# Two-layer encoder on one core: the cross-attention's output projection tile by tile with parity blocks, the MLP's Strassen operands from transposed tiles, and a hand-written order for the up-projection

## The chip, the cores and the metric

The kernel runs on one core of one Trainium2 chip, in one launch. The metric is the device time in microseconds. A core has TensorE (PE: matmuls and transposes, with the weight load PEld beside it), VectorE (DVE), ScalarE (ACT), GpSimd (POOL) and SyncE (SP, whose queue issues nearly all transfers here). Each engine works through its own queue in order and waits there on semaphores of the others; PSUM has eight banks of 128x512 f32 that PE writes and DVE or ACT read.

## The reference

An encoder of two layers over 1024 tokens of width 1024. Layer 0 mixes tokens by attention, layer 1 by pooling; each layer then cross-attends into 256 memory tokens and ends in a gated MLP of inner width 2816 with a convolution of width 3 along the tokens. The part that the change touches:

```python
def memory_cross_attention(h, mem_n, w_q, w_kv, w_o):
    ...
    o = jnp.einsum('bhsm,bmhd->bshd', p, v).reshape(b, s, D_MODEL)
    return o @ w_o

def conv_gated_ffn(h, w_up, conv_w, conv_b, w_down):
    u = h @ w_up
    up = jnp.pad(u, ((0, 0), (1, 1), (0, 0)))
    u = up[:, :-2] * conv_w[0] + up[:, 1:-1] * conv_w[1] + up[:, 2:] * conv_w[2] + conv_b
    gate, val = u[..., :D_FF], u[..., D_FF:]
    return (jax.nn.silu(gate) * val) @ w_down
...
        x = x + memory_cross_attention(rmsnorm(x, xattn_norm[i]), rmsnorm(mem, mem_norm[i]),
                                       xattn_w_q[i], xattn_w_kv[i], xattn_w_o[i])
        x = x + conv_gated_ffn(rmsnorm(x, ffn_norm[i]), ffn_w_up[i], ffn_conv_w[i],
                               ffn_conv_b[i], ffn_w_down[i])
```

## The kernel before

**Products.** All matrices are float32. `hi_lo` splits an operand in two reduced parts: ACT writes the high part (L153), DVE subtracts it to get the low part (L154). `mm3` multiplies two split operands with three matmuls, high by high, high by low and low by high (L233, L234, L235). The parts live in `R`, 20 tiles that are given out whole or by halves; raw data and intermediate results live in six `scr` tiles. `psB` hands out single PSUM banks in turn, `psA` pairs of banks.

**Stages of a layer.** Mixer; `cross`, which ends with the transposed attention output `O` in blocks of four token tiles; output projection; up-projection; down-projection. The residual `X` is eight tiles of 128 tokens by 1024 channels.

**Output projection (`project`, L248).** An outer loop goes over the two halves `n` of 512 output columns, an inner one over the eight token tiles `t`. A step is eight `mm3` into one bank and a DVE add into `X` (L261). The weight half is loaded and split at the start of its `n`. In the second round each finished tile gets `first(t)`: a DMA of the raw residual to DRAM (`Xd<-X`, L723) and the RMS norm in place (L219); one tile later `second(t)` prepares the operands of the MLP.

**Operands of the up-projection (`seven_into`, L706).** For each pair f of 22, the gate block f and the value block 22 + f of 128 columns each are computed together as a 2 by 2 block product in Strassen's form as modified by Winograd: seven products instead of eight. On the token side, the blocks of X are split by first and last four token tiles and by lower and upper 512 channels; on the weight side, the blocks are A11, A12, A21, A22. In the code's names, p1 = A11·B11, p2 = A12·B21, p3 = S4·B22, p4 = A22·T4, p5 = S1·T1, p6 = S2·T2, p7 = S3·T3. B and T blocks are made from X in row layout: subtractions first (L733, two on DVE and two on POOL, with a tile `extra`), then every block is transposed on PE (`turn`, L718) and split. T3 and T4 are turned after the projection (`tail`). That makes 112 transposes of 128x128 a layer. The S blocks are sums of weight blocks, made by POOL (L782 to L785).

**Up-projection (`ffn`, `ffn_main`).** `load(f)` brings the two 512 KB weight blocks of pair f (L771). A product is four `mm3`, so twelve matmuls (`product`). The bank `z` holds p1, then p6, p7 and p4 on top of it; the bank `y` holds p5, then p3. After each product its bank is read into `u`: p2 is copied by ACT (L811), p1 is added by DVE (L817), p5 and p6 are copied by ACT (p6's at L879), p3 is added (L885), p7 is added (L890), p4 is copied by ACT (L896). `z` may not be continued before it has been read. Then the width-3 convolution runs over u: centre tap on ACT (L841), left and right taps on DVE (L842, L843); SiLU on ACT (L887); the gate product on DVE (L902); the result G goes to DRAM (L903). Pair f's products are written in the order p1, p5, p6, p3, p7, p2 of pair f + 1, p4, with `ahead()` placing the splits of pair f + 1 between them. The order in which the engines get all this is set by the framework's scheduler, in the projection and in the whole up-projection.

**Down-projection (L910 to L938).** It reads G back and multiplies in rounds of four blocks. It starts once the up-projection has ended.

Of the kernel before, what the change touches and what calls it, by code (L numbers as in the profile page):

```python
# [16 lines left out]
P = 128  # L17
# [13 lines left out]
XH = 4  # L31
# [49 lines left out]
class Slots:  # L81
# [31 lines left out]
    def hv(self, h):  # L113
        return self.tiles[h[0]][:, h[1] * 1024:(h[1] + 1) * 1024]


class Kernel:
# [504 lines left out]
    def cross(self, i, hT, qT, ws):  # L622
# [19 lines left out]
        def scores(t):  # L642
# [19 lines left out]
            if t % 4 == 3:  # L662
                for h in range(XH):
                    R.put(qT[h, half])

        def turn(t):
            if t % 4 == 0:
                PT[t // 4] = [R.get() for _ in range(4)]
            self.transposed(prs.pop(t), self.put_T(PT[t // 4], t))
# [17 lines left out]
        for t in range(4):  # L687
            scores(t)
            memory_part(4 + t)
        for t in range(4):  # L690
            scores(4 + t)
            turn(t)
        values(0, (0, 1))
        turn(4)
        values(0, (2, 3))
        turn(5)
        turn(6)
# [8 lines left out]
    def seven_into(self, X, gain, Xd):  # L706

        nc, R = self.nc, self.R  # L710
        H = {}

        def turn(name, t, src):
            if name not in H:
                H[name] = [R.get(), R.get()]
            p = self.psB().rearrange("p (a b) -> p a b", a=4)
            for k in range(4):
                nc.tensor.transpose(p[:, k, :], src[:, k * P:(k + 1) * P], self.ident)  # L718
            h, l = (R.v(s, 4)[:, :, (t % 4) * P:(t % 4 + 1) * P] for s in H[name])
            self.hi_lo(h, l, p)  # L720

        def first(t):
            nc.sync.dma_start(out=Xd[t * P:(t + 1) * P, :], in_=X[t])  # L723
            self.normed(X[t], gain, X[t])

        def second(t):
            lo, hi = slice(0, 512), slice(512, 1024)
            if t < 4:
                turn("B11", t, X[t][:, lo])
                turn("B21", t, X[t][:, hi])  # L730
                return
            x, y = X[t - 4], X[t]
            sub = lambda e, out, p, q: e.tensor_tensor(out=out, in0=p, in1=q, op=OP.subtract)  # L733
            sub(nc.vector, x[:, lo], y[:, lo], x[:, lo])
            t2 = self.extra
            sub(nc.vector, t2, y[:, hi], x[:, lo])
            sub(nc.gpsimd, y[:, lo], y[:, hi], y[:, lo])
            sub(nc.gpsimd, x[:, hi], x[:, hi], t2)
            turn("B22", t, y[:, hi])
            turn("T1", t, x[:, lo])  # L740
            turn("T2", t, t2)

        def tail():
            for t in range(4, NT):
                turn("T3", t, X[t][:, :512])
            for t in range(4, NT):
                turn("T4", t, X[t - 4][:, 512:])
        return (first, second), H, tail

    def ffn(self, i, H, X, Xd):  # L750
        nc, R, a = self.nc, self.R, self.a
# [4 lines left out]
        cp = self.psB()[:, :4 * 2 * NF].rearrange("p (j f) -> p j f", j=4)  # L756
        for j in range(4):
            nc.tensor.transpose(cp[:, j, :], c3[:, j, :], self.ident[:2 * NF, :2 * NF])
        cv = self.cst.tile([P, 4, 2 * NF], F32, name="conv")
        nc.vector.tensor_copy(cv, cp)  # L760
        wu, wd = a["ffn_w_up"][i], a["ffn_w_down"][i]
        G = self.tc.dram_tile([FF, S], F32, name=f"G{i}")
        raws, ops, bank = {}, {}, {}
        spare = []

        def load(f):

            tiles = [spare.pop(0) for _ in range(4)] if spare else [self.scr() for _ in range(4)]
            for j, c in ((0, f), (1, NF + f)):
                src = wu[:, c * P:(c + 1) * P].rearrange("(k p) n -> p k n", p=P)  # L770
                nc.sync.dma_start(out=tiles[j].rearrange("p (k n) -> p k n", k=NK), in_=src)  # L771
            raws[f] = tiles

        def blocks(f):
            g, v, s, u = raws[f]
            return {"A11": g[:, :512], "A12": g[:, 512:], "A21": v[:, :512], "A22": v[:, 512:],
                    "S1": s[:, :512], "S2": s[:, 512:], "S3": u[:, :512], "S4": u[:, 512:]}

        def sums(f):
            b = blocks(f)  # L780
            tt = nc.gpsimd.tensor_tensor
            tt(out=b["S1"], in0=b["A21"], in1=b["A22"], op=OP.add)  # L782
            tt(out=b["S2"], in0=b["S1"], in1=b["A11"], op=OP.subtract)
            tt(out=b["S4"], in0=b["A12"], in1=b["S2"], op=OP.subtract)
            tt(out=b["S3"], in0=b["A11"], in1=b["A21"], op=OP.subtract)  # L785

        def halves(h):
            return R.hv(h)[:, :512], R.hv(h)[:, 512:]

        def split(f, name):  # L790
            h = ops[f, name] = R.get_half()
            self.hi_lo(*halves(h), blocks(f)[name])

        def done(f):
            if f:
                spare.extend(raws[f])
            del raws[f]

        def product(f, left, right, out, start):

            ah, al = (x.rearrange("p (k n) -> p k n", k=4) for x in halves(ops[f, left]))
            bh, bl = (R.v(s, 4) for s in H[right])
            for k in range(4):
                self.mm3(out, ah[:, k], al[:, k], bh[:, k], bl[:, k], start and k == 0, k == 3, not start)
            R.put_half(ops.pop((f, left)))

        def p2(f):
            x = self.psB()
            product(f, "A12", "B21", x, True)
            u = bank[f] = {"g": self.scr()}  # L810
            nc.scalar.copy(u["g"][:, :512], x)  # L811

        def p1(f):
            u = bank[f]
            z = u["z"] = self.psB()
            product(f, "A11", "B11", z, True)
            nc.vector.tensor_tensor(out=u["g"][:, :512], in0=z, in1=u["g"][:, :512], op=OP.add)  # L817

        load(0)
        sums(0)  # L820
        for n in ("A12", "A11", "S1", "S2"):
            split(0, n)

        def go():
            p2(0)
            p1(0)

        return go, lambda late, tail: self.ffn_main(H, X, Xd, late, tail, cv, G, wd, spare, load, sums, split, done,
                                                    product, p1, p2, bank)

    def ffn_main(self, H, X, Xd, late, tail, cv, G, wd, spare, load, sums, split, done, product, p1, p2, bank):
        nc, R = self.nc, self.R
        tail()
        for n in ("S4", "S3", "A22"):
            split(0, n)
        done(0)
        spare.extend(X[t] for t in (4, 5, 6, 7, 0, 1, 2, 3))

        def conv(u, f):
            c = self.scr()  # L840
            nc.scalar.activation(c, u, AF.Identity, scale=cv[:, 1, f:f + 1], bias=cv[:, 3, f:f + 1])  # L841
            nc.vector.scalar_tensor_tensor(c[:, 1:], u[:, :S - 1], cv[:, 0, f:f + 1], c[:, 1:], op0=OP.mult, op1=OP.add)  # L842
            nc.vector.scalar_tensor_tensor(c[:, :S - 1], u[:, 1:], cv[:, 2, f:f + 1], c[:, :S - 1], op0=OP.mult, op1=OP.add)  # L843
            return c
# [12 lines left out]
        order = ("A12", "A11", "S1", "S2", "S4", "S3", "A22")  # L857
        load(1)
        sums(1)
        for f in range(NF):  # L860
            u, left = bank[f], list(order)

            def ahead(n=1):
                for _ in range(n):
                    if f + 1 < NF:
                        if left:
                            split(f + 1, left.pop(0))
                            if not left:
                                done(f + 1)
                    elif first:  # L870
                        operand(*first.pop(0))

            if f:
                p1(f)
                ahead()
            z, y = u["z"], self.psB()
            product(f, "S1", "T1", y, True)
            u["v"] = self.scr()
            nc.scalar.copy(u["v"][:, 512:], y)  # L879
            ahead()  # L880
            product(f, "S2", "T2", z, False)
            nc.scalar.copy(u["g"][:, 512:], z)
# [22 lines left out]
        for s in H.values():  # L905
            R.put(*s)
# [239 lines left out]
```

## Time and profile before

| | |
|---|---|
| time, median of 3 runs | 2661.28 us (2661.01 to 2662.27) |
| time of the profiled execution | 2661.13 us |
| span of the profile | 2659.4 us |
| PE busy | 2595.0 us, 98% |
| DVE, ACT, POOL busy | 1720.5, 1207.8, 695.0 us |
| mean granted clock of TensorE | 0.992 |

In layer 0, the output projection and the first pairs of the up-projection run from 846 us to 1055 us of the span and the rest of the up-projection up to 1389 us; in layer 1 the same stages begin at about 1925 us. A row of the timeline gives the start, the duration, the engine, the line, the operation, output and input with their shapes, and in brackets how long the engine was idle before it and what ended that. Busy time is no start-to-start time: DVE and ACT begin an instruction before the one ahead has fully ended, and PE's matmuls overlap. So what an instruction takes of its queue is read as the distance of two starts. The granted clock is the share of TensorE's full clock in a stretch.

### The profile page before, as it was taken

How to read it: one execution, taken by the hardware profiler on the slowest of the kernel's cores; microseconds unless marked ns; L12 is line 12 of the kernel's file. 1: busy time of each engine (PE TensorE's matmuls, PEld its weight loads, DVE VectorE, ACT ScalarE, POOL GpSimd, SP SyncE). 2: the span in 40 equal slices, each digit the busy share in tenths (PEclk: the TensorE clock that was granted, in tenths of full speed). 3: DMA queues.
4: the chain of work that ended last, by engine and by line, in shares of the span. 5: the costliest groups of instructions: out<-in, count | busy, mean ns of one | idle time of the engine just before them, and what ended most of it. 6: DMA issues, size and time to landing. Idle time of an engine off the chain costs nothing.

```text
span 2659.4 us, 36296 instructions
## 1 busy us (share of the span) xinstructions
PE 2595.0 (98%) x13913; PEld 2216.8 (83%) x13913; DVE 1720.5 (65%) x2291; ACT 1207.8 (45%) x2024; POOL 695.0 (26%) x709
## 2 busy tenths in 40 slices
PE   8989999999999999999999998999999999999998
PEld 7988888888898878888878888889878888887886
DVE  6779999955246387777765435425378777767434
ACT  4448888843135255454542205425245555444111
POOL 3664445521012153433300001102034333310001
PEclk9999999999999999999999999999999999999999
DMA  4200000032222132223254203322122232326201
GB/s 157 83 1 1 1 1 1 2 135 65 70 80 89 48 95 73 94 72 95 87 187 154 100 19 89 103 64 72 58 92 91 72 95 72 95 104 241 99 24 63
DMA packets 167554, 209.22 MB, mean 79 GB/s; under 512 B 6741, under 2 KB 134077, under 8 KB 167381
## 3 DMA queue, kind: packets, MB, share of 16 engines
q1 hardware_dynamic: 167381, 206.91, 23.4%
q8 instruction: 109, 1.79, 0.3%
q14 instruction: 64, 0.52, 0.1%
HBM read 166.42 MB, written 35.65 MB: 76 GB/s over the span
## 4 chain that ended last, share of the span: by engine, by line
PE 57%; DVE 2%; ACT 2%; DMA 1%; issue 1%; POOL 1%; SPq 0%; POOLq 0%; DVEq 0%; ACTq 0%
PE pB L234 18%; PE pB L233 18%; PE pB L235 18%; DVE R L154 1%; ACT R L153 1%; DMA scr<-X 0%; DMA scr<-G 0%; PE pA L998 0%; PE pA L233 0%; PE pA L234 0%; PE pA L235 0%; DVE scr L842 0%; PE pB L718 0%; POOL ms L206 0%; DVE scr L843 0%
## 5 line engine op out<-in xcount | busy, mean ns | idle before, releaser
L233 PE MATMUL pB<-R,R 128*128 128x512 f32 (+1 forms) x3088 | 1160.9, 377 | 16.5 <-ACT scr L879 9.6
L234 PE MATMUL pB<-R,R 128*128 128x512 f32 (+1 forms) x3088 | 1157.6, 375 | 4.3 <-DVE R L154 4.0
L235 PE MATMUL pB<-R,R 128*128 128x512 f32 (+1 forms) x3008 | 1125.6, 374 | 0.0
L233 PEld LDWEIGHTS pB<-R,R 128*128 128x128 f32 x3088 | 582.1, 189 | 127.6 <-ACT scr L879 10.4
L234 PEld LDWEIGHTS pB<-R,R 128*128 128x128 f32 x3088 | 582.7, 189 | 109.0 <-DVE R L154 7.5
L235 PEld LDWEIGHTS pB<-R,R 128*128 128x128 f32 x3008 | 567.5, 189 | 101.0 <-DVE R L154 0.4
L153 ACT ACTIVATE R<-scr 128x1024 fp32r<-128x1024 f32 (+1 forms) x186 | 185.7, 1024 | 353.0 <-PE pB L234 283.5
L154 DVE TENSOR_TENSOR R<-X,R 128x512 fp32r<-128x512 f32 x294 | 256.3, 885 | 63.6 <-ACT R L153 63.0
L153 ACT ACTIVATE R<-X 128x512 fp32r<-128x512 f32 x294 | 181.3, 630 | 245.4 <-PE pB L234 225.6
L922 DVE TENSOR_TENSOR X<-pB,X 128x512 f32<-128x512 f32 x192 | 130.9, 688 | 221.3 <-PE pB L235 221.2
L206 POOL TENSOR_SCALAR ms<-ss 128x1 f32<-128x1 f32 (+2 forms) x102 | 26.8, 263 | 909.0 <-ACT scr L214 422.4
L154 DVE TENSOR_TENSOR R<-scr,R 128x1024 fp32r<-128x1024 f32 (+1 forms) x186 | 218.0, 1194 | 49.5 <-ACT R L153 46.2
L153 ACT ACTIVATE R<-pB 128x512 fp32r<-128x512 f32 (+1 forms) x216 | 113.8, 556 | 185.3 <-PE pB L235 81.3
L227 PE MATMUL pB<-ident,scr 128*128 128x128 f32 x1376 | 182.4, 276 | 9.7 <-DVE scr L219 8.0
L227 PEld LDWEIGHTS pB<-ident,scr 128*128 128x128 f32 x1376 | 157.5, 142 | 36.5 <-POOL scr L319 14.6
L319 POOL TENSOR_SCALAR scr<-scr,inv 128x1024 f32<-128x1024 f32 x128 | 144.0, 1125 | 167.2 <-DVE inv L318 162.3
L154 DVE TENSOR_TENSOR R<-pB,R 128x512 fp32r<-128x512 f32 (+1 forms) x216 | 131.4, 636 | 76.9 <-ACT R L153 76.3
L842 DVE SCALAR_TENSOR_TENSOR scr<-scr,conv 128x1023 f32<-128x1023 f32 x88 | 139.4, 1584 | 62.4 <-ACT scr L841 62.0
L782 POOL TENSOR_TENSOR X<-X 128x512 f32<-128x512 f32 x42 | 56.2, 1339 | 447.0 <-DMA X<-in_ffn_w_up 447.0
L154 DVE TENSOR_TENSOR PT<-pB,PT 128x512 fp32r<-128x512 f32 x256 | 163.9, 680 | 3.3 <-ACT PT L153 2.4
L316 ACT ACTIVATE scr<-pA,nm 128x1024 f32<-128x1024 f32 x128 | 142.9, 1116 | 44.6 <-DVE nm L313 42.6
L313 DVE TENSOR_REDUCE nm<-pA 128x1 f32<-128x1024 f32 x128 | 156.1, 1220 | 0.9 <-PE pA L309 0.5
(123 smaller groups left out, 3188.7 us busy)
## 6 DMA issues: line engine op xcount, KB each, us to landing
X<-in_ffn_w_up SPq DMA_DIRECT2D x84, 512.0 KB
G<-scr SPq DMA_DIRECT2D x44, 512.0 KB
scr<-G SPq DMA_DIRECT2D x44, 512.0 KB
scr<-in_ffn_w_down SPq DMA_DIRECT2D x44, 512.0 KB
scr<-in_xattn_w_kv SPq DMA_DIRECT2D x32, 512.0 KB
scr<-in_attn_w_qkv SPq DMA_DIRECT2D x20, 512.0 KB
scr<-in_xattn_w_q SPq DMA_DIRECT2D x16, 512.0 KB
scr<-in_xattn_w_o SPq DMA_DIRECT2D x16, 512.0 KB
```

What stands on the lines that cost most here:

```text
L153: nc.scalar.activation(hi, src, AF.Copy)
L154: nc.vector.tensor_tensor(out=lo, in0=src, in1=hi.bitcast(F32), op=OP.subtract)
L227: self.nc.tensor.transpose(p[:, k, :], src[:, b * P:(b + 1) * P], self.ident)
L233: mm(out, ah, bh, start=start, stop=False)
L234: mm(out, ah, bl, start=False, stop=False)
L235: mm(out, al, bh, start=False, stop=stop)
L313: nc.vector.tensor_reduce(nm, s, axis=AX.X, op=OP.max, negate=True)
L316: nc.scalar.activation(pr, s, AF.Exp, bias=nm, accum_out=rs)
L319: nc.gpsimd.tensor_scalar(pr, pr, ri, 1.0, op0=OP.mult, op1=OP.mult)
L782: tt(out=b["S1"], in0=b["A21"], in1=b["A22"], op=OP.add)
L842: nc.vector.scalar_tensor_tensor(c[:, 1:], u[:, :S - 1], cv[:, 0, f:f + 1], c[:, 1:], op0=OP.mult, op1=OP.add)
L922: nc.vector.tensor_tensor(out=x, in0=p, in1=x, op=OP.add)
```

## The change

The stages before `cross` of layer 0 stay as they are, and so do the matmuls of all products. What is different:

- **Blocks by parity.** The token tiles are split in even and odd (t % 2, t // 2) instead of first and last four, in `cross`'s transposes, in `O`, and in the token blocks of the up-projection. `cross` takes its tiles in another order to fit.
- **Output projection.** Both weight halves are loaded and split at the start. Sixteen steps (n, t) are written out by hand in `begin`, each finished tile's row being stored, normed and turned between them.
- **Operands from transposed tiles.** Only X itself is turned: eight transposes for each of eight tiles, 64 a layer. Subtractions take place on the transposed blocks, straight from PSUM: three by DVE for each odd tile (`take1`), a fourth by POOL or DVE (`fourth`). `extra` is gone.
- **Weight sums.** The four sums of a pair are made by DVE (`sums`).
- **Order of the up-projection.** From the projection up to pair 20 the order is written by hand (`manual_schedule`): `begin` covers pair 0 and the head of pair 1, then each pair follows a list; pairs 1, 2 and 3 (`second`, `third`, `fourth`) have lists of their own, and pairs 4 to 20 share `steady`. In a list each product is followed by what is issued after it, `read` being the read of its bank. Pair 21 is left to the scheduler.
- p2 writes a bank of `psA`. The reads of banks write strided halves of u, since a block is now every second tile. The convolution table is turned in its own function.

```diff
+class Seven:
...
+    def take1(self, t):
+        nc, ps, lo, hi = self.nc, self.ps[t], self.LO, self.HI
+        x, y = self.X[t - t % 2], self.X[t]
+        nc.scalar.copy(y[:, lo], ps[0])
+        if t % 2:
+            self.sub(nc.vector, x[:, lo], ps[0], x[:, lo])
+            self.sub(nc.vector, y[:, hi], ps[1], x[:, lo])
+            self.sub(nc.vector, y[:, lo], ps[1], y[:, lo])
...
+    def sums(self, f, *which):
...
+            self.nc.vector.tensor_tensor(out=b[n], in0=b[p], in1=b[q], op=op)
...
+    def begin(self, gemm, add, free, between, gate):
+        late, split = self.late, self.split
+        steps = ((0, 0), (0, 2), (1, 0), (1, 2), (0, 4), (1, 4), (0, 6), (1, 6),
+                 (0, 1), (1, 1), (0, 3), (1, 3), (0, 5), (0, 7), (1, 5), (1, 7))
+        turns = {3: 0, 4: 2, 6: 4, 8: 6, 10: 1, 12: 3, 15: 5}
...
+        for i, (n, t) in enumerate(steps):
+            gemm(n, t)
+            free(n, t)
+            u = turns.get(i)
+            if u is not None:
+                self.turn(u)
+            extras.get(i, lambda: None)()
+            add(n, t)
+            if n:
+                self.rows(t)
+            if u is not None:
+                self.take1(u)
+            if n:
+                self.norm(t)
+            if u is not None:
+                self.take2(u)
...
+        read[7]()
+        read[3]()
+        read[4] = self.p4(0)
+        self.sums(1, "S1")
+        split(1, "S1")
+        read[5] = self.p5(1)
+        self.sums(1, "S2")
+        split(1, "S2")
+        read[4]()
...
+        self.sums(1, "S4", "S3")
+        split(1, "S4")
+        read[5]()
...
+        ws = [self.load_rows(w, n) for n in range(2)]
...
+        steady = ((U.p1, load, split(A12), ahead, back(V1), read), (U.p5, split(A11), ahead, back(V2), read),
+                  (U.p6, split(S1), ahead, back(gated), read), (U.p3, split(S2), sums(1, S4, S3), ahead, read, G0),
+                  (U.p7, split(S4), ahead, read, G1), (p2, split(S3), G2, read, silu),
+                  (U.p4, split(A22), done, ahead, sums(2, S1, S2), read, V0))
+        second = ((U.p6, here(S3, A22), lambda f: U.done(f), back(G1), read),
+                  (U.p3, split(A12), back(G2), back(silu), back(V0), read),
+                  (U.p7, split(A11), back(V1), read, G0),
+                  (p2, load, sums(1, S1), split(S1), back(V2), read),
+                  (U.p4, sums(1, S2), split(S2), back(gated), read, V0))
+        third = ((U.p1, sums(0, S4), here(S4), back(G1), read), (U.p5, sums(0, S3), here(S3), back(G2), read, back(silu)),
+                 (U.p6, here(A22), lambda f: U.done(f), load, back(V1), read), (U.p3, split(A12), back(V2), read, G0),
+                 (U.p7, split(A11), back(gated), read, G1), (p2, sums(1, S1), split(S1), G2, read, silu),
+                 (U.p4, sums(1, S2), split(S2), read, V0))
+        fourth = ((U.p1, sums(0, S4), here(S4), back(V1), read), (U.p5, sums(0, S3), here(S3), back(V2), read),
+                  (U.p6, here(A22), lambda f: U.done(f), load, split(A12), back(gated), read), (U.p3, split(A11), sums(1, S1, S2), read, G0),
+                  (U.p7, split(S1, S2), read, G1), (p2, sums(1, S4, S3), split(S4), G2, read, silu),
+                  (U.p4, split(S3, A22), done, sums(2, S1, S2), read, V0))
+
+        def pair(f, todo):
+            for product, *then in todo:
+                reading = product(f) if product is not p2 or f + 1 < NF else lambda: None
+                for what in then:
+                    what(f) if what else reading()
+
+        with self.tc.manual_schedule():
+            begin((lambda: G0(0),))
+            for f in range(1, NF - 1):
+                pair(f, {1: second, 2: third, 3: fourth}.get(f, steady))
+        pair(NF - 1, steady)
```

Here G0, G1, G2 are the centre, left and right taps of the gate half of u, V0, V1, V2 those of the value half; `back` takes the pair before, `here` splits operands of the same pair, `split` those of the next; `sums(1, ...)` and `sums(2, ...)` make sums one and two pairs ahead.

More of the change, by code (lines that the diff above doesn't have):

```diff
@@ L703, in cross, with conv_table @@
         return O
[L706 to L751, printed above, removed]
+    def conv_table(self, i):
+        nc, a = self.nc, self.a
         cw = self.scr()
@@ L763, in ffn @@
[L763 to L844, printed above, removed]
+        def turn():
+            cp = self.psB()[:, :4 * 2 * NF].rearrange("p (j f) -> p j f", j=4)
+            for j in range(4):
+                nc.tensor.transpose(cp[:, j, :], c3[:, j, :], self.ident[:2 * NF, :2 * NF])
+            self.cv = self.cst.tile([P, 4, 2 * NF], F32, name="conv")
+            nc.vector.tensor_copy(self.cv, cp)
@@ L905, in ffn_main, with sums, split, ahead @@
-        for s in H.values():
+        A12, A11, S1, S2, S4, S3, A22 = "A12", "A11", "S1", "S2", "S4", "S3", "A22"
+        p2 = lambda f: U.p2(f + 1)
+        def sums(n, *names):
+            return lambda f: f + n < NF and U.sums(f + n, *names)
+        def split(*names):
+            return lambda f: f + 1 < NF and U.split(f + 1, *names)
+        def ahead(f):
+            if f == NF - 1:
+                operand(*first.pop(0))
+        def load(f):
+            if f + 2 < NF:
+                U.load(f + 2)
@@ L1100, in late @@
                     ready["pool"] = self.pool_weights()
-            rest, done = ready["ffn"](late, tail)
+            rest, done = self.ffn(i, a["xattn_w_o"][i], lhs, X, free, late)
             if i == 0:
```

295 lines of the change are left out of this document (223 added, 72 removed).

## The prediction

> **What bounds the kernel now.** I read the busy table first, then the chain of work that ended last, the waits of TensorE (PE), the windows around the changed stages, and the timeline.
>
> ```profile
> span 2659.4 us, 36296 instructions
> PE 2595.0 (98%) x13913; PEld 2216.8 (83%) x13913; DVE 1720.5 (65%) x2291; ACT 1207.8 (45%) x2024; POOL 695.0 (26%) x709
> ...
> PE 57%; DVE 2%; ACT 2%; DMA 1%; issue 1%; POOL 1%; SPq 0%; POOLq 0%; DVEq 0%; ACTq 0%
> ...
> PE pB L233 <- ACT scr L879: 9.6, 2, 4.8
> ```
>
> PE is the bound: only fewer matmuls or fewer waits of PE shorten the kernel. Its largest group here is two waits of 4.8 us, one in each layer, on the put of pair 0's third block. The next windows (columns: stretch, its length, busy time of PE, weight load, DVE, ACT and POOL, granted clock) cover layer 0 from the first output-projection matmul to the end of pair 4; then pairs 5 onward; then what follows the long wait.
>
> ```profile
> 846.20:1055.20 209.00, 202.44 (x934) 166.68 (x933) 133.84 (x148) 79.06 (x127) 72.45 (x56) 0.98 0.22 70
> 1055.20:1360.00 304.80, 304.80 (x1344) 251.59 (x1343) 225.52 (x236) 151.86 (x221) 96.55 (x56) 1.00 0.28 90
> 965.30:971.30 6.00, 5.93 (x15) 4.67 (x16) 6.00 (x6) 2.18 (x5) 4.48 (x3) 0.54 0.28 83
> ```
>
> The first stretch has idle time and a dip of the clock. In the second PE waits for nothing, so the steady pairs can only lose.
>
> **The change part by part.** First the unit of each piece of PE work.
>
> ```profile
> 851.87 0.69 DVE L261 TENSOR_TENSOR X<-pB,X 128x512 f32<-128x512 f32 x1 [1.59 <-PE pB L235]
> 857.31 0.69 DVE L261 TENSOR_TENSOR X<-pB,X 128x512 f32<-128x512 f32 x1 [4.75 <-PE pB L235]
> ...
> 907.40 1.03 PE L718 MATMUL pB<-ident,X 128*128 128x128 f32 x8
> 908.19 0.48 PE L233 MATMUL pB<-R,R 128*128 128x512 f32 x1
> ...
> 965.37 0.79 PE L233 MATMUL pB<-R,R 128*128 128x512 f32 x1 [4.84 <-ACT scr L879]
> ...
> 1047.25 0.69 DVE L885 TENSOR_TENSOR scr<-pB,scr 128x512 f32<-128x512 f32 x1 [1.66 <-PE pB L235]
> 1066.29 0.69 DVE L885 TENSOR_TENSOR scr<-pB,scr 128x512 f32<-128x512 f32 x1 [1.66 <-PE pB L235]
> 1067.02 1.25 ACT L841 ACTIVATE scr<-scr,conv 128x1024 f32<-128x1024 f32 x1 [0.33 <-DVE scr L885]
> ...
> L758 PE MATMUL pB<-ident,scr 44*128 44x44 f32 x4 | 0.4, 238 | 0.0
> ```
>
> An output-projection tile takes 5.44 us (857.31 − 851.87); eight transposes 0.79; a pair 19.04, so a product 19.04/7 = 2.72. The stretch holds 16 tiles, 36 products (pairs 0 to 4 and pair 5's first) and 112 transposes: 16 × 5.44 + 36 × 2.72 + 14 × 0.79 + 0.4 for the conv table = 196.4. Of 209.0 us, 12.6 are lost: 4.84 in the wait, 6.00 × 0.46 = 2.8 in the slow clock behind it, the rest in short waits.
>
> *Transposes.* Turning only X takes 64 a layer, 48 fewer: 6 × 0.79 = −4.7 us.
>
> *The 4.84 us wait.* The hand-written order puts that read ahead of most splits, so I take the whole 12.6 away and count the waits of the new order instead, from the built queues, with these rows as prices.
>
> ```profile
> 833.11 0.68 DVE L154 TENSOR_TENSOR R<-pB,R 128x512 fp32r<-128x512 f32 x1
> 833.85 0.50 PE L233 MATMUL pB<-R,R 128*128 128x512 f32 x1 [0.81 <-DVE R L154]
> ...
> 1054.94 0.57 ACT L811 COPY scr<-pB 128x512 f32<-128x512 f32 x1
> 1055.40 1.16 ACT L153 ACTIVATE R<-X 128x512 fp32r<-128x512 f32 x2
> 1056.07 0.69 DVE L154 TENSOR_TENSOR R<-X,R 128x512 fp32r<-128x512 f32 x1 [1.59 <-ACT R L153]
> 1056.45 0.58 ACT L896 COPY scr<-pB 128x512 f32<-128x512 f32 x1
> 1057.07 1.25 ACT L841 ACTIVATE scr<-scr,conv 128x1024 f32<-128x1024 f32 x1
> 1058.22 0.61 ACT L153 ACTIVATE R<-X 128x512 fp32r<-128x512 f32 x1
> ...
> 1096.24 1.28 DVE L842 SCALAR_TENSOR_TENSOR scr<-scr,conv 128x1023 f32<-128x1023 f32 x1 [0.98 <-ACT scr L841]
> 1097.44 0.68 DVE L817 TENSOR_TENSOR scr<-pB,scr 128x512 f32<-128x512 f32 x1
> 1098.04 1.28 DVE L843 SCALAR_TENSOR_TENSOR scr<-scr,conv 128x1023 f32<-128x1023 f32 x1
> ...
> 1099.83 1.22 DVE L902 TENSOR_TENSOR scr<-scr 128x1024 f32<-128x1024 f32 x1
> 1100.97 0.69 DVE L154 TENSOR_TENSOR R<-X,R 128x512 fp32r<-128x512 f32 x1
> ...
> 1356.37 1.27 DVE L843 SCALAR_TENSOR_TENSOR scr<-scr,conv 128x1023 f32<-128x1023 f32 x1
> 1357.73 1.06 ACT L887 ACTIVATE scr<-scr 128x1024 f32<-128x1024 f32 x1 [3.21 <-DVE scr L843]
> 1358.70 0.57 ACT L811 COPY scr<-pB 128x512 f32<-128x512 f32 x1
> ...
> L887 ACT ACT_TABLE_LOAD x2 | 2.6, 1283 | 1.5 <-DVE scr L843 1.4
> ```
>
> Start to start: put 0.46; ACT half of a split to its DVE half 0.67, to the next ACT instruction 0.53 (1.05/2); put to a dependent conv centre 0.62, conv 1.15; DVE 128x512 0.60; a conv tap 1.20; the gate 1.14; last tap to SiLU 1.36, SiLU 0.97; the table load 1.28; a DVE read to the PE product behind it 0.74, plus 0.11 for the restart (0.34 from 833.85 to the next matmul, not 0.23: an estimate); a DVE result to a dependent ACT instruction 0.73 (1067.02 − 1066.29). A product's end to its read is 0.20, an estimate from PE's modelled ends.
>
> Each pair's products share a bank: p6 waits for p1's read, p4 for p7's, and those reads stand in DVE's queue behind conv taps, splits and now the sums. Added along the built order, against the PE work meanwhile (from a read it has 0.85 + 3 products = 9.01, or + 4 = 11.73):
> - Pair 0, p4: p7's read at once: 0.20 + 0.74 + 0.11 = 1.05.
> - Pair 1, p4, from p6's end: put 0.20 + 0.46, split 0.67 + 0.60, tap to the table load 1.36 + 1.28, SiLU 0.97, conv 1.15, split 0.67 + 0.60, tap 1.20, read 0.74 = 9.90 against 8.16: with the restart 1.85.
> - Pair 2, p6, from p7's read: 0.60, S1 sum and split 0.73 + 0.67 + 0.60, tap 1.20, S2 sum and split 2.00, gate 1.14, S4 sum and split 2.00, tap 1.20, read 0.74 = 10.88 against 9.01: 1.98.
> - Pair 2, p4: 0.60, S3 sum and split 2.00, tap to SiLU 1.36, 0.97, split 0.67 + 0.60, tap 1.20, 0.60, tap 1.20, p3's read 0.73, conv 1.15, split 0.67 + 0.60, gate 1.14, 0.74 = 14.23 against 11.73: 2.61.
> - Pair 3, p6: 0.60, tap 1.20, S1 2.00, tap to SiLU 1.36, 0.97, ACT 0.53, put 0.62, conv 1.15, split 0.67 + 0.60, tap 1.20, 0.74 = 11.64 against 9.01: 2.74. Pair 3, p4: 12.56 in the same way (tap, gate, four splits, three sums, p3's read, conv) against 11.73: 0.94.
> - Pair 4, p6: 0.60, tap 1.20, two sums 1.33, split 0.67 + 0.60, tap to SiLU 1.36, 0.97, two ACT halves 1.06, put 0.62, conv 1.15, split 0.67 + 0.60, tap 1.20, 0.74 = 12.77 less 0.60, since the S3 sum runs beside S4's ACT half: 12.17 against 9.01: 3.27.
>
> *Turns in the projection.* Each tile's transposes now come one tile after its add:
>
> ```profile
> 895.39 0.69 DVE L261 TENSOR_TENSOR X<-pB,X 128x512 f32<-128x512 f32 x1 [4.75 <-PE pB L235]
> 896.11 0.35 SPq L723 DMA_DIRECT2D Xd<-X  x1
> 899.65 1.28 DVE L219 SCALAR_TENSOR_TENSOR X<-X,rs,scr 128x1024 f32<-128x1024 f32 x1 [3.57 <-DMA Xd<-X]
> 900.99 0.33 PE L718 MATMUL pB<-ident,X 128*128 128x128 f32 x1 [0.20 <-DVE X L219]
> ```
>
> Tile end to transposes is 0.20 + (900.99 − 895.39) = 5.80 against 5.44: a wait of 0 to 0.36 plus restart, as this DMA goes. I take 0.25 for seven of eight turns: 1.75.
>
> *Sum of this stretch:* waits 1.75 + 1.05 + 1.85 + 1.98 + 2.61 + 2.74 + 0.94 + 3.27 = 16.2; −4.7 − 12.6 + 16.2 = −1.1 a layer.
>
> *Steady pairs, 5 to 20.* In source order with the split ahead of each read, and S4's and S3's sums on DVE, a loop runs from p6's end to the next p6: put 0.20 + 0.46, S2 split 0.67, its DVE half and two sums 1.80, p3's read 0.73, conv 1.15, S4 split 0.67 + 0.60, p7's read 0.60, tap 1.20, S3's DVE half 0.60, tap to SiLU 1.36, SiLU 0.97, A22 0.53, put 0.62, conv 1.15, A12 split 0.67 + 0.60, the value tap 1.20, p1's read 0.74 = 16.52. PE has six products between, 16.32. So p6 comes 0.20 + 0.11 = 0.3 late in each of 16 pairs: +4.8. Bounds: 0 (now) and 0.6.
>
> *Costed at nothing.* The sums taken off POOL, which ends no wait here; their DVE time is in the loop above. Both weight halves loaded at the start, needed 11 us apart by two tiles. Loads of later weights, issued on SP's queue at p1 and first read by DVE's sums six products, 16.3 us, later; a store of the same 512 KB was through in 3.5 us (896.11 to 899.65). If one landed late, the sum at the head of DVE's queue would hold p1's read behind it, and PE with that. Cross's new tile order: as many instructions. The end of the up-projection, still left to the scheduler.
>
> **Total:** 2 × (−1.1 + 4.8) = +7.4; against the profiled execution's 2661.13 us (span 2659.4 with what lies around it; 0.15 under the median of 2661.28) that is 2668.5, taken as 2668. I assume that both layers pay alike.
>
> **The rivals.**
> *A, the queue sum:* 2668; own range 2663 to 2676 (±20% on the waits and 0.2 to 0.45 per pair).
> *B, the steady loop fits:* it is 0.20 long in twenty steps, so 0.01 a step closes it; then 2661.1 − 2.2 = 2659. For it: PE's complete windows above. Against: there the scheduler picked the order, and POOL had the sums.
> *C, the hand-offs are shorter, and the kernel faster:* the changed order runs with POOL silent, and the group of splits, partly with POOL beside it, has a longer mean (885 ns):
>
> ```profile
> L154 DVE TENSOR_TENSOR R<-X,R 128x512 fp32r<-128x512 f32 x294 | 256.3, 885 | 63.6 <-ACT R L153 63.0
> ```
>
> My price goes with the short ones of 0.69 us (1056.07), which speaks against C. The six waits' chains add to 71.4 us a layer. With 2% off, the steady loop fits and the waits lose 1.4: 2 × (−1.1 − 1.4) = −5, 2656: there it turns faster. With 5%: −3.6, 2652. With 10%: −6.8 (one wait is gone before), 2645.
> *D, long waits slow the clock:* the 4.84 us wait halved it for 6 us, 2.8 us lost. The three waits of 2.6 to 3.3 us in pairs 2 to 4 may do so too; one or two per layer: 2668 + 2 × 2.8 or 4 × 2.8 = 2674 to 2679. A shorter wait, and the clock (0.54) at its end:
>
> ```profile
> 1609.76 0.56 PE L998 MATMUL pA<-scr 128*128 128x112 f32 x1 [3.94 <-ACT scr L991]
> ...
> 1609.00:1610.00 1.00, 0.24 (x1) 0.24 (x2) 0.00 (x0) 0.71 (x1) 0.00 (x0) 0.54 0.77 213
> ```
>
> The Trainium skill, "TensorE: Matmul & The Clock Gate", section "What's actually happening", puts the loss of clock at an idle window of about 3.4 us. By that rule 3.27 stays just short, the windows being free-running, and D fails; the waits of 4.84 and 3.94 us agree, and no row quoted here tests 3.3.
>
> **How the numbers follow.** Chances: A 0.42, B 0.14, C 0.28, D 0.16. What can be told from no change is about 0.2%, 5.3 us: faster is below 2656, slower above 2666. Faster: C 0.26, B 0.06, A 0.02 = 0.34. Same: B 0.08, A 0.04, C 0.02 = 0.14. Slower: A 0.36, D 0.16 = 0.52. The range runs from C at 12%, 2642, to D with the steady loop at 0.45, 2679 + 2 × 16 × 0.15 = 2684.
>
> **What would show it.** In the changed profile: 64 transposes a layer; no 4.8 us wait on the put; waits of PE on DVE of about 1 to 3 us in pairs 0 to 4, first products p4 and p6; in steady pairs reads of p3 spaced 19.3 us, with p6 waiting each time for p1's read. Spacing of 19.04 means B or C; a clock near 0.5 within pairs 2 to 4 means D. The forecast is wrong if those waits are half as long, or if PE waits in steady pairs for a load or the sums.

## The result, and the profile after

| | before | after |
|---|---|---|
| median | 2661.15 us (4 runs, 2660.63 to 2662.27) | 2676.4 us (4 runs, 2675.07 to 2678.22) |
| ratio, 95% interval | | 1.0057 (1.004 to 1.0075) |
| time and span of the profiled execution | 2661.13, 2659.4 us | 2676.43, 2674.7 us |

The kernel became 15 us slower; 2668 was forecast, with a range of 2642 to 2684. The page of the changed kernel and the top of its table of PE's waits (total, times, longest):

```profile
span 2674.7 us, 35818 instructions
PE 2595.4 (97%) x13817; PEld 2207.0 (83%) x13817; DVE 1733.5 (65%) x2479; ACT 1214.0 (45%) x2048; POOL 375.9 (14%) x521
...
PE pB L478 <- DVE scr L238: 23.5, 13, 3.0
```

The two waits of 4.8 us on a put are gone. In their place stand 13 waits on L238, which is DVE's read of a bank (`add`). PE's timeline shows where they lie in layer 0, in order: p4 of pair 0, p4 of pair 1, p6 and p4 of pair 2, p6 of pair 3, p6 of pair 4.

```profile
966.07 0.47 PE L478 MATMUL pB<-R,R 128*128 128x512 f32 x1 [0.88 <-DVE scr L238]
984.23 0.50 PE L478 MATMUL pB<-R,R 128*128 128x512 f32 x1 [1.57 <-DVE scr L238]
995.02 0.47 PE L478 MATMUL pB<-R,R 128*128 128x512 f32 x1 [2.33 <-DVE scr L238]
...
996.67 0.63 PE L478 MATMUL pB<-R,R 128*128 128x512 f32 x1
997.09 0.63 PE L479 MATMUL pB<-R,R 128*128 128x512 f32 x1
...
1008.30 0.50 PE L478 MATMUL pB<-R,R 128*128 128x512 f32 x1 [0.50 <-DVE scr L238]
...
1019.24 0.47 PE L478 MATMUL pB<-R,R 128*128 128x512 f32 x1 [2.48 <-DVE scr L238]
...
1042.87 0.47 PE L478 MATMUL pB<-R,R 128*128 128x512 f32 x1 [2.72 <-DVE scr L238]
```

These are six of the seven places that the queue sum named; the seventh, p4 of pair 3, waits only in layer 1 (0.56 us). Behind these waits of 2.3 us and more the matmuls stand 0.42 us apart (996.67 to 997.09) and not 0.227: the clock is halved for a while. The windows (columns as in the prediction; the clock is the third figure from the end) show that, and the last of them lies in the steady pairs; below it are SiLUs of two steady pairs, the first add of the output projection, and the read of pair 4's p3.

```profile
990.00:1015.00 25.00, 22.17 (x89) 17.53 (x88) 17.73 (x23) 10.56 (x16) 0.00 (x0) 0.93 0.24 84
1015.00:1040.00 25.00, 22.52 (x92) 17.95 (x90) 19.24 (x27) 12.38 (x19) 0.00 (x0) 0.93 0.28 86
1040.00:1065.00 25.00, 22.28 (x91) 17.96 (x91) 18.77 (x25) 11.17 (x18) 0.00 (x0) 0.93 0.27 84
1090.00:1350.00 260.00, 258.81 (x1129) 210.57 (x1128) 196.88 (x253) 127.43 (x189) 0.00 (x0) 1.00 0.26 85
...
1076.58 1.06 ACT L1020 ACTIVATE scr<-scr 128x1024 f32<-128x1024 f32 x1 [1.05 <-DVE scr L1012]
1095.96 1.06 ACT L1020 ACTIVATE scr<-scr 128x1024 f32<-128x1024 f32 x1 [1.05 <-DVE scr L1012]
...
853.56 0.69 DVE L979 TENSOR_TENSOR X<-pB,X 128x512 f32<-128x512 f32 x1 [2.63 <-PE pB L480]
...
1050.31 0.69 DVE L238 TENSOR_TENSOR scr<-pB,scr 128x512 f32<-128x512 f32 x1
```

A steady pair takes 19.38 us (1095.96 − 1076.58) where most pairs took 19.04 before: 0.34 us more. From pair 4's read of p3 to pair 20's the changed kernel takes 310.2 us in each layer and the kernel before took 305.3: 4.9 us, so 9.7 in two layers. From the first add to pair 4's read of p3 it is 1050.31 − 853.56 = 196.8 us against 1047.25 − 851.87 = 195.4 before, 1.4 us more, and in layer 1 197.2 against 195.2, 1.9 more: 3.3 together. The first projection tile ends 1.7 us later than before (853.56 against 851.87), from a wait at 30 us of the span and slower matmuls behind it, in code that the change does not touch (see the last section). Of the 15.3 us between the spans, 15.3 − 9.7 − 3.3 − 1.7 = 0.6 remain for all other stages.

### The profile page after: what moved, and what is told of

It reads as the page before. It is cut to its first block, busy times and chain, and to the rows that moved or that the text cites. A ratio compares the mean times of both kernels' runs of the same rounds, so it can differ in the third digit from the quotient of the medians.

```text
span 2674.7 us, 35818 instructions
## 1 busy us (share of the span) xinstructions
PE 2595.4 (97%) x13817; PEld 2207.0 (83%) x13817; DVE 1733.5 (65%) x2479; ACT 1214.0 (45%) x2048; POOL 375.9 (14%) x521
## 4 chain that ended last, share of the span: by engine, by line
PE 75%; DVE 11%; ACT 5%; issue 3%; POOL 2%; DMA 2%; SPq 0%; DVEq 0%; ACTq 0%; POOLq 0%
PE pB L478 20%; PE pB L479 20%; PE pB L480 20%; PE pB L472 3%; DVE nm L558 2%; PE pA L554 2%; DVE R L399 2%; PE pA L478 2%; PE pA L480 2%; PE pA L479 2%; ACT R L398 1%; PE pB L785 1%; DVE PT L399 1%; POOL qn L630 1%; PE pB L786 1%
## 5 line engine op out<-in xcount | busy, mean ns | idle before, releaser
L478 PE MATMUL pB<-R,R 128*128 128x512 f32 (+1 forms) x2912 | 1096.2, 378 | 31.5 <-DVE scr L238 23.5
L479 PE MATMUL pB<-R,R 128*128 128x512 f32 (+1 forms) x2912 | 1090.1, 375 | 4.3 <-DVE R L399 4.0
L480 PE MATMUL pB<-R,R 128*128 128x512 f32 (+1 forms) x2832 | 1057.5, 374 | 0.0
L478 PEld LDWEIGHTS pB<-R,R 128*128 128x128 f32 x2912 | 549.8, 189 | 147.8 <-issue 35.3
L479 PEld LDWEIGHTS pB<-R,R 128*128 128x128 f32 x2912 | 550.7, 189 | 101.7 <-DVE R L399 7.3
L480 PEld LDWEIGHTS pB<-R,R 128*128 128x128 f32 x2832 | 535.1, 189 | 94.7 <-DVE R L399 0.2
L399 DVE TENSOR_TENSOR R<-X,R 128x512 fp32r<-128x512 f32 x322 | 222.7, 697 | 199.2 <-ACT R L398 199.1
L398 ACT ACTIVATE R<-X 128x512 fp32r<-128x512 f32 x322 | 192.0, 622 | 49.8 <-DVE X L208 43.7
L1002 ACT ACTIVATE scr<-scr,conv 128x1024 f32<-128x1024 f32 x88 | 109.6, 1245 | 105.6 <-DVE scr L238 101.3
L398 ACT ACTIVATE R<-pB 128x512 fp32r<-128x512 f32 (+1 forms) x184 | 95.8, 552 | 131.6 <-PE pB L480 82.2
L399 DVE TENSOR_TENSOR R<-pB,R 128x512 fp32r<-128x512 f32 (+1 forms) x184 | 110.0, 627 | 63.9 <-ACT R L398 63.4
L554 PE MATMUL pA<-R,R 128*128 128x512 f32 x512 | 146.7, 408 | 0.0
```

What stands on the lines that cost most here:

```text
L398: nc.scalar.activation(hi, src, AF.Copy)
L399: nc.vector.tensor_tensor(out=lo, in0=src, in1=hi.bitcast(F32), op=OP.subtract)
L478: mm(out, ah, bh, start=start, stop=False)
L479: mm(out, ah, bl, start=False, stop=False)
L480: mm(out, al, bh, start=False, stop=stop)
L554: nc.tensor.matmul(s[:, kh * 512:(kh + 1) * 512], q, R.v(K[part][kh], 4)[:, kv], start=part == 0, stop=part == 1)
```

## The experiments

All ratios are to the kernel before, run on the same chip. The runs were made in sets on different chips; the kernel before had medians of 2660.2 to 2661.15 us in them, so medians of different sets can be compared to about 1 us.

| run | median us | ratio (95%) |
|---|---|---|
| p1_read_first | 2657.81 | 0.9994 (0.9984 to 1.0004) |
| pool_sums | 2744.25 | 1.0316 (1.03 to 1.0331) |
| pool_sums_reads_first | 2741.83 | 1.0309 (1.0294 to 1.0324) |
| fill_waits | 2671.23 | 1.0044 (1.0029 to 1.0059) |
| own_order_1_to_4 | 2635.2 | 0.9904 (0.9887 to 0.992) |
| scheduler_pairs | 2637.41 | 0.9914 (0.9899 to 0.9928) |
| more_transposes | 2682.33 | 1.0083 (1.0068 to 1.0098) |
| scheduler_pool_sums | 2655.44 | 0.9982 (0.9973 to 0.9991) |
| own_order_more_transposes | 2642.63 | 0.9938 (0.9924 to 0.9951) |

**One read moved in the steady pairs (p1_read_first).**

```diff
-        steady = ((U.p1, load, split(A12), ahead, back(V1), read), ...
+        steady = ((U.p1, load, split(A12), ahead, read, back(V1)), ...
```

> Changed kernel, only that in the steady pairs p1's bank is read ahead of the value half's left tap, not behind it. If the steady wait is the queue loop (put, splits, sums, taps, then p1's read), 1.20 us leave the loop of 16.5 against 16.3 us of PE work: the SiLU spacing falls from 19.38 to 19.04 us in pairs 5 to 20, and pair 4's p6 waits 1.2 us less; 2 x (16 x 0.345 + 1.2) = 13 us less than 2676, so about 2663. Rival: the 0.35 us per pair come from slower operations or from bank traffic that order does not change; spacing stays near 19.38 and the time near 2676.

Measured: 2657.81, 18.6 us less. Two SiLUs of steady pairs, and the wait of pair 4's p6:

```profile
1091.44 1.06 ACT L1020 ACTIVATE scr<-scr 128x1024 f32<-128x1024 f32 x1 [1.05 <-DVE scr L1012]
1110.48 1.06 ACT L1020 ACTIVATE scr<-scr 128x1024 f32<-128x1024 f32 x1 [1.05 <-DVE scr L1012]
...
1040.47 0.47 PE L478 MATMUL pB<-R,R 128*128 128x512 f32 x1 [1.51 <-DVE scr L238]
```

19.04 us a pair, and 1.51 instead of 2.72 us at pair 4. The steady loss was the queue loop, and the rival falls. Some 5 us more came than the 13 forecast. The listed waits of pairs 0 to 4 fell by 4.9 us over both layers (23.5 to 18.6) and not by 2.4, and with 1.51 us there is no slow clock behind pair 4's p6; the rest is not taken apart.

**The weight sums back on POOL (pool_sums), and with the reads ahead (pool_sums_reads_first).**

```diff
-            self.nc.vector.tensor_tensor(out=b[n], in0=b[p], in1=b[q], op=op)
+            e = self.nc.vector if f < 2 else self.nc.gpsimd
+            e.tensor_tensor(out=b[n], in0=b[p], in1=b[q], op=op)
```

The second has, besides this and the edit above, the following in pairs 1 to 3:

```diff
-                  (U.p7, split(A11), back(V1), read, G0),
+                  (U.p7, split(A11), read, back(V1), G0),
...
-        third = ((U.p1, sums(0, S4), here(S4), back(G1), read), ...
+        third = ((U.p1, sums(0, S4), here(S4), read, back(G1)), ...
...
-                 (U.p7, split(A11), back(gated), read, G1), ...
+                 (U.p7, split(A11), read, back(gated), G1), ...
...
-        fourth = ((U.p1, sums(0, S4), here(S4), back(V1), read), ...
+        fourth = ((U.p1, sums(0, S4), here(S4), read, back(V1)), ...
```

> Changed kernel, only that the weight sums of pairs 2 to 21 go back to POOL. Queue theory: DVE loses four 0.60 us sums a pair, two of them inside the steady loop; steady spacing 19.04, and the waits of pairs 2 to 4 fall from about 11 to about 3.5 us a layer, with less time at half clock; 2 x (5.5 + 7.9 + 4) = 35 us less, about 2641. Rival: DVE is slowed while POOL works (the mean of the 128x512 splits goes from 0.70 back towards 0.89 us), the loop is as long as before and the time stays within 10 us of 2676 or above it.

> Both edits, and the reads of p1 and p7 in pairs 1 to 4 also ahead of the taps or the gate that stood before them. Queue theory: only pair 1's p4 (0.6 us) and pair 3's p6 (1.1 us) still wait, no steady wait, no slow clock; 2 x (5.5 + 11.5 + 4) = 42 us less, about 2635, below the kernel before. Rival (POOL slows DVE): 2655 to 2670.

Both forecasts missed, by 100 us. The groups of splits and bank reads on DVE, first in the changed kernel, then in pool_sums with PE's waits there:

```profile
L399 DVE TENSOR_TENSOR R<-X,R 128x512 fp32r<-128x512 f32 x322 | 222.7, 697 | 199.2 <-ACT R L398 199.1
L238 DVE TENSOR_TENSOR scr<-pB,scr 128x512 f32<-128x512 f32 x132 | 90.1, 684 | 6.1 <-PE pB L480 6.0
```

```profile
L400 DVE TENSOR_TENSOR R<-X,R 128x512 fp32r<-128x512 f32 x322 | 297.2, 929 | 215.1 <-ACT R L399 214.9
L239 DVE TENSOR_TENSOR scr<-pB,scr 128x512 f32<-128x512 f32 x132 | 89.8, 682 | 6.5 <-PE pB L481 6.5
...
L209 POOL TENSOR_TENSOR X<-X,X 128x512 f32<-128x512 f32 x120 | 215.0, 1804 | 6.3
...
PE pB L479 <- DVE scr L239: 81.3, 72, 4.7
```

A split, with two SBUF operands, goes from 697 to 929 ns on the mean (a mean over splits of which only some meet POOL), and POOL's sum takes 1804 ns. A bank read of the same size, whose first operand is in PSUM, stays at 682, but few of these reads meet POOL. Rows of scheduler_pool_sums (below), which has POOL's sums too, show single instructions beside them:

```profile
983.01 6.20 POOL L209 TENSOR_TENSOR X<-X,X 128x512 f32<-128x512 f32 x3
...
984.05 1.78 DVE L400 TENSOR_TENSOR R<-X,R 128x512 fp32r<-128x512 f32 x1
985.76 0.68 DVE L239 TENSOR_TENSOR scr<-pB,scr 128x512 f32<-128x512 f32 x1
986.36 1.70 DVE L1025 TENSOR_TENSOR scr<-scr 128x1024 f32<-128x1024 f32 x1
```

The split takes 1.78 us there and not 0.69, the gate 1.70 and not 1.22; the bank read keeps its 0.68. So the rival of the expectation held in kind, though its price was far too low: in pool_sums a steady pair takes 21.5 us, and PE waits 72 times on a bank read that stands in DVE's queue behind the slowed work. Another rival, that POOL's sums are late because POOL takes longer for them, falls: in the table of waits of pool_sums no instruction waits for one of POOL's sums. The Trainium skill, "SBUF — State Buffer", section "SBUF: two separate sides", says that DVE and POOL share one port pair under an exclusive lock, and that a DVE instruction with two SBUF inputs takes it against a POOL instruction that reads SBUF; the rows above agree, the read with a PSUM input being free of it.

Moving reads ahead gained 2 us here. A steady pair still takes 21.6 us: the two short waits of a pair (1.1 and 0.9 us) become one. Of three such waits in a row two are of 2.1 us; the second of them is followed by half clock, and the third is then 0.7 us. What sets the 21.6 us was not taken apart.

**Idle transposes inside the waits (fill_waits).**

```diff
+    FILL = {(2, "S2"): 20, (3, "S2"): 22, (4, "S2"): 24}
+    def fill(self, n):
+        x = self.kn.psA()[:, :P]
+        for _ in range(n):
+            self.nc.tensor.transpose(x, self.kn.ident, self.kn.ident)
...
+        if (f, left) in self.FILL:
+            self.fill(self.FILL[f, left])
```

> Changed kernel with 20, 22 and 24 idle transposes (2.0, 2.2, 2.4 us; their result is not used) on PE ahead of p6 of pairs 2, 3 and 4, inside the waits of 2.3 to 3.0 us found there. If those waits themselves drop the clock, it stays at 1.00 in pairs 2 to 4 and the matmuls behind them keep 0.227 us spacing: 5.1 us less in layer 0 and about 3.3 in layer 1, so about 2668. Rival: the clock drops there for another reason; windows stay at 0.93 and the time at 2676 or a little above.

Measured: 2671.23, 5 us less, where 8 were expected. Its windows, and pair 2's p4:

```profile
990.00:1015.00 25.00, 22.72 (x103) 18.43 (x102) 17.73 (x23) 10.96 (x16) 0.00 (x0) 0.93 0.25 85
1015.00:1040.00 25.00, 25.00 (x127) 21.11 (x126) 19.33 (x27) 12.65 (x21) 0.00 (x0) 1.00 0.30 93
1040.00:1065.00 25.00, 24.81 (x119) 20.41 (x118) 20.37 (x26) 10.90 (x18) 0.00 (x0) 1.00 0.24 77
...
1007.92 0.50 PE L487 MATMUL pB<-R,R 128*128 128x512 f32 x1 [2.14 <-DVE scr L247]
```

Where a wait was filled, the clock stays: the idle time of the waits caused the drop. But p4 of pair 2 now waits 2.14 us and not 0.50, and slows the clock itself. With the products at full speed PE reaches the next late read sooner. Inside pairs 2 to 4 DVE's and ACT's chain sets the pace, so most of what the slow clock costs is taken out of the next wait, as in pool_sums_reads_first (0.7 us instead of 2.1 behind a slow stretch). What shows in the end is, by this reading, the last such stretch, behind pair 4's p6.

**Another order for pairs 1 to 4 (own_order_1_to_4).** On top of p1_read_first, the lists `second`, `third` and `fourth` and pair 4 are replaced by one written order. Its part for pair 2 and the head of pair 3, one line a product:

```
p1.2 sum:S4.2 sum:S3.2 split:S4.2 read:p1.2 G1.1
p5.2 read:p5.2 split:S3.2 G2.1 silu.1
p6.2 V1.1 split:A22.2 done.2 load.4 read:p6.2
p3.2 split:A12.3 V2.1 read:p3.2 G0.2
p7.2 read:p7.2 gated.1 G1.2 split:A11.3
p2.3 G2.2 sum:S1.3 sum:S2.3 split:S1.3 silu.2
p4.2 read:p2.3 split:S2.3 read:p4.2 V0.2
p1.3 sum:S4.3 sum:S3.3 read:p1.3 V1.2 split:S4.3
```

> p1 read ahead of the tap in the steady pairs, as before, and another written order for pairs 1 to 4: both sums of a couple ahead of their splits, the reads of p1 and p7 ahead of taps, gates and splits, the centre taps and the table load behind splits that a product waits for; same operations, sums on DVE. Queue theory, by the same sums: no PE wait in pairs 1 to 4, where the kernel with p1 read first still had 1.74, 2.48, 0.70, 2.59 and 1.66 us of them in a layer and two stretches of half clock (1.7 us each, partly hidden in the next wait): 2 x (9 to 11) = 18 to 22 us less than 2658, about 2637. Rival: DVE and ACT have too much work there for any order (or a scr tile that comes free later makes a wait of its own): the waits move to other products and the time stays at 2650 to 2660.

Measured: 2635.2, which is 22.6 us below p1_read_first (18 to 22 expected), 41 below the changed kernel and 25.6 below the kernel before. Its waits in pairs 0 to 4 of layer 0, and two windows:

```profile
965.95 0.47 PE L478 MATMUL pB<-R,R 128*128 128x512 f32 x1 [0.88 <-DVE scr L238]
991.77 0.47 PE L478 MATMUL pB<-R,R 128*128 128x512 f32 x1 [1.09 <-DVE scr L238]
...
990.00:1015.00 25.00, 23.91 (x105) 19.26 (x105) 22.12 (x28) 13.75 (x22) 0.00 (x0) 1.00 0.29 94
1015.00:1040.00 25.00, 25.00 (x112) 20.72 (x111) 22.77 (x33) 12.99 (x20) 0.00 (x0) 1.00 0.39 127
```

One wait of 1.1 us is left in pairs 1 to 4, and the clock stays at 1.00. In the same 50 us DVE is busy for 44.9 us, against 37.0 in the changed kernel: it had the time, and the order made it idle. The rival (too much work for any order) falls.

**The scheduler for the pairs (scheduler_pairs), and with POOL's sums (scheduler_pool_sums).** The lists stay as program text; only the loop stands outside the written part:

```diff
         with self.tc.manual_schedule():
             begin((lambda: G0(0),))
-            for f in range(1, NF - 1):
-                pair(f, {1: second, 2: third, 3: fourth}.get(f, steady))
-        pair(NF - 1, steady)
+        for f in range(1, NF):
+            pair(f, {1: second, 2: third, 3: fourth}.get(f, steady))
```

> Changed kernel, but only begin is written by hand; pairs 1 to 21, with the same lists as program text and DVE sums, are ordered by the framework's scheduler. If the written order is what costs in the steady pairs, spacing is 19.04 and the time 2645 to 2665. If the DVE sums cost whatever the order, spacing stays at 19.3 or more and the time at 2676 or above.

> The kernel whose pairs 1 to 21 the scheduler orders (2637), only with the weight sums of pairs 2 to 21 on POOL again. It tells whether POOL's work hurts by itself or only together with the written order. If the scheduler's order has room for the slower DVE, as the kernel before had (splits of 0.89 us and no waits): steady spacing 19.04 and 2635 to 2645. If POOL's slowing of DVE costs in any order with these operands: spacing above 19.3 and more than 2655.

Measured: 2637.41, below both ranges that were expected, and 2655.44. Pairs 2 to 4 of scheduler_pairs, then its steady pairs:

```profile
990.00:1015.00 25.00, 25.00 (x112) 20.67 (x111) 24.98 (x35) 13.90 (x23) 0.00 (x0) 1.00 0.39 126
1015.00:1040.00 25.00, 25.00 (x112) 20.71 (x111) 23.32 (x33) 12.71 (x19) 0.00 (x0) 1.00 0.32 101
1090.00:1350.00 260.00, 258.40 (x1137) 213.01 (x1136) 192.37 (x245) 128.52 (x184) 0.00 (x0) 1.00 0.28 92
```

and the steady pairs of scheduler_pool_sums, with its splits, two of PE's waits and one of ACT's, in pairs before these:

```profile
1090.00:1350.00 260.00, 259.71 (x1144) 214.00 (x1143) 197.11 (x203) 129.09 (x189) 83.75 (x48) 1.00 0.29 91
...
L400 DVE TENSOR_TENSOR R<-X,R 128x512 fp32r<-128x512 f32 x322 | 275.1, 871 | 56.0 <-ACT R L399 55.8
...
PE pB L479 <- DVE scr L239: 8.9, 5, 3.5
PE pB L479 <- ACT R L399: 8.4, 11, 2.5
...
ACT R L399 <- POOL X L209: 20.3, 15, 2.6
```

With the scheduler's order PE has few waits in either kernel's steady pairs (two a layer in scheduler_pairs, of 0.3 to 1.9 us), so POOL's sums cost nothing there, although the splits are nearly as slow as in pool_sums. They cost 18 us all the same, in pairs 0 to 2: there PE waits up to 3.5 us on bank reads and 2.5 us on ACT's splits. Two causes meet in these pairs, DVE's slowed work and sums that are late, for ACT's splits wait there for POOL's sums (20.3 us in 15 waits); which costs more was not tried. For the second kernel each of the two expected cases was half right: the steady pairs are those of the first, the time, just, that of the second.

**Transposes doubled (more_transposes, own_order_more_transposes).**

```diff
+        for b in (0, 1, 2, 4, 5, 6):
+            self.nc.tensor.transpose(self.ps[t][b // 4][:, b % 4 * P:(b % 4 + 1) * P],
+                                     self.X[t][:, b * P:(b + 1) * P], self.kn.ident)
```

> Changed kernel with six of each token tile's eight transposes done twice, 48 more a layer, which is the number that the change took away. If they lie on PE's path: 2 x 48 x 0.099 = 9.5 us more, 2686. Rival: the waits of pairs 0 to 4 absorb part of it, since DVE and ACT get that time too: 2677 to 2682.

> The kernel with the new order of pairs 1 to 4 (2635), with 48 transposes a layer more. Nothing in its pairs 0 to 4 waits long, so nothing can absorb them: 2 x 48 x 0.099 = 9.5 us more, 2644 to 2645. If it is 6 us or less, as the medians of the earlier pair of runs had it, then transposes are cheaper than their spacing says.

Measured: 2682.33 against 2676.4 (+5.9), and 2642.63 against 2635.2 (+7.4). The first add of the projection and p4 of pair 0 in more_transposes:

```profile
854.21 0.69 DVE L982 TENSOR_TENSOR X<-pB,X 128x512 f32<-128x512 f32 x1 [2.64 <-PE pB L483]
...
971.68 0.47 PE L481 MATMUL pB<-R,R 128*128 128x512 f32 x1 [0.87 <-DVE scr L241]
```

That stretch is 971.68 − 854.21 = 117.5 us; without the extra transposes it is 966.07 − 853.56 = 112.5. So 48 transposes cost 5.0 us of PE's path, 0.104 each, in full; in layer 1, and in both layers of the other kernel, the same stretch grows by 5.0 to 5.1. The medians show less than 2 × 5.0, and the four sets of runs and their starts spread by about 2 us; the first kernel could also take some of it out of later waits, the second has none to take it from. The medians settle neither 9.5 nor 6; the stretch does.

## Why the prediction was right

The sign came out as predicted, and so did the steady pairs, which give most of the loss; the stretch before them was mis-sized. Of the 7.9 us by which the loss exceeded the forecast (15.3 against 7.4 between the spans), 5.5 lie in that stretch and 1.7 in the wait at 30 us of the span.

- *Transposes, −4.7 us a layer:* 5.0 by the doubled ones.
- *The 4.84 us wait:* gone, with the slow clock behind it.
- *Waits of the written order in pairs 0 to 4:* predicted with the restart 1.05, 1.85, 1.98, 2.61, 2.74, 0.94, 3.27. Found in layer 0, without it: 0.88, 1.57, 2.33, 0.50, 2.48, none, 2.72. All sit on the named products and on the named reads. 0.50 instead of 2.61 and the missing one at pair 3's p4 come behind stretches of half clock, which the sum left out: when these stretches were filled, 2.14 came back in the place of 0.50. In layer 1, where the clock stayed until the last wait, the list is 0.88, 1.57, 2.33, 2.15, 2.48, 0.56, 3.00, close to the sums everywhere.
- *Turns in the projection, 1.75:* not seen; PE has no wait there in layer 0.
- *The slow clock, put at nothing in the forecast case and only in rival D:* three windows of layer 0 at 0.93 lose 3 × 25 × 0.07 = 5.2 us. With the waits (10.5, and 0.7 of restarts) that is 16.4, where the forecast had 16.2 for waits alone. That the two agree is partly luck: the waits behind a slow stretch became shorter, and the turns, which cost no wait, made up the rest.
- *The stretch as a whole:* −1.1 forecast, +1.4 and +1.9 measured. The step that failed is the removal of the whole 12.6 us. Of these, the trace before lists 6.5 as waits (4.84, 0.79, 0.63 and 0.20), 2.8 is the slow clock, and 3.3 is neither; the prediction put it down to short waits. Counted in the same way, from the first add to pair 4's read of p3, the changed kernel's 196.8 us hold 15 × 5.44 + 33 × 2.72 + 8 × 0.79 + 0.4 = 178.1 of work. Of the other 18.7 us, 10.5 are waits, 5.2 the clock and 3.0 neither. So this remainder stayed: 0.7 of it are the restarts counted above, and with the other 2.3 the sum becomes −1.1 + 0.2 + 2.3 = +1.4. A part of it is in the turns: a projection step with eight transposes takes 6.3 to 6.6 us, not 5.44 + 0.79.
- *Steady pairs, 0.3 us each, +4.8 a layer:* 0.34 and +4.9, from the read of p1 behind the value tap. Moving that one read took it to zero. Rival B, that the loop just fits, falls.
- *Rival C, shorter hand-offs:* not seen; the loop was 0.04 us longer than the sum, not shorter.
- *Rival D, the clock:* came, at shorter waits than the 3.9 us that the prediction could quote. The time lies in its band, 2674 to 2679, and just beyond A's own range, but not in the way that D priced it: what the slow clock cost was in good part made up by shorter waits behind it. The Trainium skill, "TensorE: Matmul & The Clock Gate", section "What's actually happening", has the clock fall after an idle window of about 3.4 us; by that figure these waits of 2.3 to 3.0 us would not have slowed it. The trace differs, and decides.
- *Costed at nothing, the sums off POOL:* the work itself ended no wait, but it was not nothing. With the sums on POOL the kernel takes 18 us more in the scheduler's order and 68 more in the written one. The change gained this, and the forecast did not count it apart, because its prices were taken from rows that POOL did not disturb.
- *Loads, cross's order, weight halves, at nothing:* no wait of PE on them stands out.
- *Both layers pay alike:* steady pairs yes. In layer 1 of the changed kernel the waits differ as the clock does.

What the change is worth by parts, then: with the scheduler ordering the pairs, operands from transposed tiles, the projection and DVE's sums give 2661 − 2637 = 24 us; writing out the pairs in this order costs 39 us, more than all of it, and 18.6 of the 39 go with one misplaced read.

## What to carry to other kernels

When operations move into a written order, add up each loop that runs through several in-order queues and compare it with the PE work in the same loop: here 0.2 us too much in 16.3 showed as 0.34 us in each of 32 pairs, and a bank's read that frees the next product belongs ahead of work that nobody waits for. When a loss is taken away whole in a forecast, list what it is made of first. Try the scheduler on the same program text before keeping a written order. Before moving elementwise work to an idle POOL, look whether DVE's instructions with two SBUF operands lie on the critical loop, and whether the result can come later.

## What the runs showed of the hardware that was not expected

- Short waits can halve TensorE's clock. Waits of 2.33, 2.48 and 2.72 us in layer 0 of the changed kernel were each followed by matmuls at 0.42 us spacing for some 3 us, beginning 1.1 to 1.2 us after PE had gone on; 2.14 us did it in fill_waits. Waits of 0.9 and 1.6 us did not, nor did this one in layer 1 of the changed kernel, at full clock in the window that holds it:

```profile
2031.57 0.47 PE L478 MATMUL pB<-R,R 128*128 128x512 f32 x1 [2.33 <-DVE scr L238]
...
2030.00:2055.00 25.00, 19.58 (x84) 15.61 (x84) 18.05 (x23) 10.38 (x15) 0.00 (x0) 1.00 0.20 64
```

  Two waits of scheduler_pool_sums are equally long; the first, in layer 0, left the clock at 1.00, and behind the second, in layer 1, it was 0.63:

```profile
1010.41 0.50 PE L479 MATMUL pB<-R,R 128*128 128x512 f32 x1 [3.49 <-DVE scr L239]
1010.00:1014.00 4.00, 3.59 (x16) 2.95 (x17) 3.67 (x3) 1.94 (x3) 4.00 (x3) 1.00 0.09 25
...
2035.91 0.69 PE L479 MATMUL pB<-R,R 128*128 128x512 f32 x1 [3.49 <-DVE scr L239]
2035.00:2039.00 4.00, 3.09 (x8) 2.45 (x9) 4.00 (x4) 1.45 (x3) 4.00 (x3) 0.63 0.20 53
```

  So between about 2.1 and 3.5 us it may go either way; what decides it was not found.
- DVE instructions with two SBUF operands are slowed by POOL's (a split from 0.69 to 1.78 us), one with an operand in PSUM was not (0.68 beside POOL).
- A wait of PE near 30 us of the span, in code that all these kernels share, was 1.30 us in the profile before and 2.71 in the profile after:

```profile
30.03 0.39 PE L235 MATMUL pB<-T,R 128*128 128x256 f32 x1 [1.30 <-DVE R L154]
```

```profile
30.52 0.58 PE L480 MATMUL pB<-T,R 128*128 128x256 f32 x1 [2.71 <-DVE R L399]
```

  In the other kernels' profiles it lies between 1.22 and 2.84; what sets it was not tried.
